# A retrieval trunk's gate one-hots and gate products: one one-hot moved from GpSimd to VectorE, multiplies and loads of gates placed by tile

## The chip, the cores and the metric

The kernel runs on one core of a Trainium2 chip. The metric is the device time of one execution in microseconds (us). Engines are named as in the profile: PE (TensorE, with PEld for its weight loads), DVE (VectorE), ACT (ScalarE), POOL (GpSimd) and SP (SyncE, whose queue SPq issues most transfers). Each engine works through its own queue in order; engines wait for each other by semaphores.

## What is computed

Two layers over 512 tokens of 1024 channels, in float32. Each layer has a mixing part (a convolution module with gated linear attention, then forgetting attention) and an expert-retrieval part (PEER), which this change touches. Of the reference:

```python
PEER_HEADS, PEER_NKEYS, PEER_TOPK = 8, 128, 16      # 128 x 128 = 16384 experts
def peer_ffn(h, wq, keys, u, v):
    ...
    sc, j = lax.top_k(cand, PEER_TOPK)
    e1 = jnp.take_along_axis(i1, j // PEER_TOPK, axis=-1)
    e2 = jnp.take_along_axis(i2, j % PEER_TOPK, axis=-1)
    experts = e1 * PEER_NKEYS + e2
    gates = jax.nn.softmax(sc, axis=-1)
    ...
    def block(args):
        ht, et, gt = args
        act = jax.nn.gelu(jnp.einsum('td,ted->te', ht, u[et]), approximate=False)
        return jnp.einsum('te,ted->td', gt * act, v[et])
```

Every token picks 128 experts (8 heads, 16 each). An expert has a number `e1 * 128 + e2`, a row of `u` that is dotted with the token, and a row of `v` that is added with the weight gate times gelu(dot).

## The kernel before

The 512 tokens are four blocks of 128. Block 0 is done by gathering: its 128 `u` rows per token come by indirect transfers that POOL issues (`g_u`, L861, a [128, 1024] tile `gr` each, one per slot), DVE dots them with `h` (L863); later the `v` rows come the same way (`g_v`, L872) and DVE adds them to `x` with their weights (L874). The other three blocks (384 tokens, `TD`) are done densely: all 16384 experts are computed, as 128 expert tiles of 128 (index `e1`, `NE1`), and a dense gate matrix, zero where a token did not pick an expert, masks them.

**u steps** (`u_step`). For one tile of 128 experts the weight tile `raw` (512 KB) is loaded by SP into one of 4 buffers. Matmuls are done with a high and a low half: ACT makes the high half `whi` (L50), DVE the low half `wlo` (L51), three buffers each. PE then does 8 x 3 matmuls `pu` (L77 to L79) against the tokens' own halves; ACT takes the gelu (L853). The last 24 tiles' activations stay in SBUF (`act0` and so on), the other 104 are put by in DRAM (`aside`).

**The gate stage.** From u step 36 to 116, `gate4` makes the dense gates, four tokens at a time, 96 times a layer. For a token, the matrix [e2, e1] is the product of two one-hot matrices over its 128 slots. DVE makes the one-hots over e2 of four tokens at once (`a2`, L898, [128, 512]). The four gate-weighted one-hots over e1 (`a1`, [128, 128] each) are shared out: POOL makes tokens 0 and 1 and DVE token 2 (L901), ACT token 3 with two activations (L904, L905). PE multiplies them (L911, behind a u step's matmuls; six groups of four fall to five u steps), ACT copies the result into `big` (L912), and for every 16 tokens SP writes `big` to `G` in DRAM (L914, 1 MB). `a1` and `a2` have three buffers. In the same stretch POOL issues about 1.4 row gathers for each u step, five buffers `gr`.

**The v sweep.** For tile n (0 to 127, the 24 with kept activations first) `prepare` loads and splits the `v` weights as above and makes the weights per token: gates `gc`, a block of 1.5 MB for 8 tiles (L957, two buffers), times the activations (L969, [128, 384], in place), split into `wh` (ACT) and `wl` (DVE). The activations that were put by return as `at`, two tiles a load (L960, three buffers). PE does 18 matmuls `acc` (L1025) a tile. `fetch(n)` issues the loads of `gc` and `at`; the sweep calls it AHEAD = 4 tiles before their use.

**What sets the order.** The program is written in this sequence, but a scheduler with a simulated timeline decides where each instruction stands in its engine's queue, as soon as its operands and buffers are free by that simulation. `tc.issue_after(x)` adds an edge: what is traced inside stands behind `x` on that engine. `self.last_lo` is the last low half that `split` made.

Of the kernel before, what the change touches and what calls it, by code (L numbers as in the profile page):

```python
# [4 lines left out]
F32 = mybir.dt.float32  # L5
# [6 lines left out]
ALU = mybir.AluOpType  # L12
# [4 lines left out]
P = 128  # L17
# [5 lines left out]
NE1 = 128  # L23
# [6 lines left out]
TG = 16  # L30
NTG = TD // TG
EC = 8
KEEP = 24
ROWS = 5
LAG = 2
AHEAD = 4
# [8 lines left out]
class Trunk:  # L45
# [768 lines left out]
    def peer_body(self, L, hT, h0, sp, sb):  # L814
        nc, tc, A = self.nc, self.tc, self.A
# [4 lines left out]
        G = self.dp.tile([NTG, P, NE1 * TG], F32, name="G")  # L820
# [12 lines left out]
        def pump(q, n):  # L833

            done = []
            for _ in range(min(int(n), len(q))):
                f, args = q.pop(0)
                done.append(f(*args))
            return [f for f in done if f]


        def u_step(e, eng=None):
            wh, wl = self.weight(uT[e], (KD, P), eng)
            if e % 2 and HEADS * WQU <= e < NE1 - 2:
                p = self.bank([P, TD], "pu")
            else:
                p = self.ps.tile([P, TD], F32, tag="b", name="pu", bufs=2)
            lo = self.last_lo
            for k in range(KD):
                mm = self.mm3(p, wh[:, k], wl[:, k], hD[0][:, k], hD[1][:, k], k == 0, k == KD - 1)  # L850
            put_by = e < NE1 - KEEP
            a = sb.tile([P, TD], F32, name="xact", bufs=3) if put_by else kept[e - (NE1 - KEEP)]
            self.last_gelu = nc.scalar.activation(a, p, AF.Gelu)  # L853
            if put_by:
                nc.sync.dma_start(aside[e], a)
            return lo, mm
# [27 lines left out]
        def flip(b):  # L884
            p = self.bank([P, 3, P])
            for j, t in enumerate((E[:, 0, DB[b]], E[:, 1, DB[b]], S[:, DB[b]])):
                nc.tensor.transpose(p[:, j], t.rearrange("p h k -> p (h k)"), self.ident)
            nc.scalar.activation(sT[b][:, 0:3], p, AF.Copy)
            nc.scalar.activation(sT[b][:, 3], p[:, 2], AF.Copy, scale=-1.0)

        def gate4(ub, b, tg, g):
            t0 = tg * TG + 4 * g
            if g == 0:
                self.big = ub.tile([P, NE1, TG], F32, name="big", bufs=2)
            a2 = ub.tile([P, 4, P], F32, name="a2", bufs=3)
            a1 = ub.tile([P, 4, P], F32, name="a1", bufs=3)
            e1, e2, gate, step = (sT[b][:, k, t0:t0 + 4] for k in range(4))
            nc.vector.tensor_tensor(a2, self.iota[:, None, :].to_broadcast([P, 4, P]),  # L898
                                    e2[:, :, None].to_broadcast([P, 4, P]), op=ALU.is_equal)
            for t in range(3):  # L900
                (nc.vector if t == 2 else nc.gpsimd).tensor_scalar(a1[:, t], self.iota, e1[:, t:t + 1], gate[:, t:t + 1],  # L901
                                                                   op0=ALU.is_equal, op1=ALU.mult)

            nc.scalar.activation(a1[:, 3], self.iota, AF.Abs, scale=-1.0, bias=e1[:, 3:4])  # L904
            nc.scalar.activation(a1[:, 3], a1[:, 3], AF.Relu, scale=step[:, 3:4], bias=gate[:, 3:4])  # L905
            big = self.big

            def multiply():
                p = self.bank([P, 4, P])
                for t in range(4):  # L910
                    nc.tensor.matmul(p[:, t], a2[:, t], a1[:, t], start=True, stop=True)  # L911
                nc.scalar.activation(big[:, :, g * 4:g * 4 + 4].rearrange("p e t -> p t e"), p, AF.Copy)  # L912
                if g == TG // 4 - 1:
                    nc.sync.dma_start(G[b * (P // TG) + tg], big.rearrange("p e t -> p (e t)"))  # L914

            return multiply
# [3 lines left out]
        with tc.tile_pool(name=f"pr{L}", bufs=2, reuse_waits="tile") as rb:  # L920
            for hd in range(HEADS):
                qT = []
                for w in range(2):
                    p = self.proj_T(A["wq"][L, 2 * hd + w], hT, nc.gpsimd if w and hd else None,
                                    after=None if hd else self.last_sq)
# [6 lines left out]
                for b in range(NB):  # L932
                    p = self.bank([P, 2, P])
# [13 lines left out]
        order = [*range(NE1 - KEEP, NE1), *range(NE1 - KEEP)]  # L947
        gcs, ats = {}, {}

        def fetch(n):  # L950

            if n >= NE1:
                return
            e = order[n]
            if n % EC == 0:
                gcs[n] = vb.tile([P, NTG, EC * TG], F32, name="gc")
                nc.sync.dma_start(gcs[n], G[:, :, e * TG:(e + EC) * TG].rearrange("g p n -> p g n"))  # L957
            if e < NE1 - KEEP and n % 2 == 0:
                ats[n] = vb.tile([P, 2, TD], F32, name="at", bufs=3)
                nc.sync.dma_start(ats[n], aside[e:e + 2].rearrange("e p t -> p e t"))  # L960

        def prepare(n):

            e, r = order[n], n % EC
            a = kept[e - (NE1 - KEEP)] if e >= NE1 - KEEP else ats[n - n % 2][:, n % 2]
            vh, vl = self.weight(vN[e], (2, 512))
            lo = self.last_lo
            w = gcs[n - r][:, :, r * TG:(r + 1) * TG]
            nc.vector.tensor_tensor(w, w, a.rearrange("p (g t) -> p g t", t=TG), op=ALU.mult)  # L969
            wh = vb.tile([P, TD], F32R, name="wh", bufs=3)  # L970
            wl = vb.tile([P, TD], F32R, name="wl", bufs=3)
            self.split(w, *[t.rearrange("p (g t) -> p g t", t=TG) for t in (wh, wl)])
            return lo, (n, vh, vl, wh, wl)
# [9 lines left out]
        vpool = tc.tile_pool(name=f"pv{L}", bufs=2, reuse_waits="tile")  # L983
        ub, vb = upool.__enter__(), None
        gates = [(gate4, (ub, b, tg, g)) for b, tg in groups for g in range(TG // 4)]
        while nu < NE1:
            if vb and nu == NE1 - 1:
                ready.append(prepare(0))
            lo, mm = u_step(nu)
            nu += 1  # L990
            with tc.issue_after(mm.ins):
                for f in products:
                    f()
                if nu == first:
                    for b in range(nd):
                        flip(b)
            products = []
            if nu >= first:
                cg += ng
                products = pump(gates, cg)  # L1000
                cg -= int(cg)
            if not (gates or products or vb):
                upool.__exit__(None, None, None)
                vb = vpool.__enter__()
                for n in range(AHEAD):
                    fetch(n)
            with tc.issue_after(lo.ins):
                for f in rows.pop(0):
                    f()
            cq += nq  # L1010
            rows.append(pump(gathers, cq))
            cq -= int(cq)
        assert vb and not (gates or products or gathers or any(rows))
        ready.append(prepare(1))
        g_w()

# [14 lines left out]
        for n in range(NE1):  # L1031
            fetch(n + AHEAD)
            lo, tile = ready.pop(0) if ready else prepare(n)
            tail.append(tile)
            if n < NE1 - 3:
                for b in range(nd):
                    v_sweep(tail, b)
                tail.clear()
            with tc.issue_after(lo.ins):
                for f in rows.pop(0):  # L1040
                    f()
            cq += nq
            rows.append(pump(gathers, cq))
            cq -= int(cq)
            if not gathers and not any(rows) and not done:
                done = True
                g_end()
# [124 lines left out]
```

## Time and profile before

| | |
|---|---|
| median of 3 runs | 3236.9 us (3230.26 to 3238.59) |
| the profiled execution | 3237.96 us |
| its span (first to last instruction) | 3236.2 us |
| mean granted PE clock | 0.985 |
| gate stage, layers 0 and 1 | from 543.9 and 2183.6 us on, first `L911` |
| v sweep, layers 0 and 1 | first `acc` matmuls at about 1045 and 2688, last at about 1585 and 3231 us |

The span holds everything between the first and the last instruction; 1.8 us of the execution lie outside it. Rows of the profile name a source line, an engine, an operation and output<-input by the program's names; `xN` is a count. In a table of windows each engine has its busy time in that stretch, then come the clock granted to PE (1.00 is full), the share of the 16 transfer engines that is busy, and GB/s. In a wait row the numbers are total us, times, longest. "Chain" is the work that ended last, followed back step by step to what released it.

### The profile page before, as it was taken

The page shows a single profiled execution, that of the slowest core. Times are in us where ns is not written, and L with a number is a line of the kernel's source. Part 1 is how long each engine was busy: PE and PEld are TensorE (multiplying, and loading weights), DVE is VectorE, ACT ScalarE, POOL GpSimd, SP SyncE. Part 2 cuts the span into 40 slices and gives each one's busy share as a digit, 9 for nine tenths or more (in the row PEclk, how much of TensorE's full clock was granted, in tenths as well). Part 3 has the DMA queues.
Part 4 walks back from the last instruction along what each step waited for, and adds up shares of the span by engine and source line. Part 5 has one row for each costly group of instructions (what it writes and reads, how often), then busy time and mean ns, then how long its engine had stood idle before and what let it go on. Part 6 is the DMA issues. An engine that isn't in the chain of part 4 may idle for free.

```text
span 3236.2 us, 45689 instructions
## 1 busy us (share of the span) xinstructions
PE 3112.4 (96%) x15932; PEld 2712.8 (84%) x15932; DVE 2361.4 (73%) x4744; ACT 1440.8 (45%) x2258; POOL 1416.7 (44%) x992
## 2 busy tenths in 40 slices
PE   8999999899999999999999999998999999999999
PEld 6768998899999788877766679998999998788787
DVE  7765988677676788878545639886776767788886
ACT  4353334566564333333356623345665643333333
POOL 1310124999994343333100001229999963443340
PEclk9999999999999999999999999998999999999999
DMA  4113445899899899999421124448998897999996
GB/s 153 57 37 123 145 138 188 310 325 329 307 326 308 277 343 373 359 334 347 143 79 46 33 90 143 139 164 283 334 321 313 308 319 273 325 369 353 350 350 215
DMA packets 334201, 787.15 MB, mean 243 GB/s; under 512 B 26745, under 2 KB 181770, under 8 KB 327826
## 3 DMA queue, kind: packets, MB, share of 16 engines
q1 hardware_dynamic: 260242, 515.76, 46.6%
q0 software_dynamic: 73728, 268.47, 23.4%
q8 instruction: 125, 2.05, 0.3%
q14 instruction: 106, 0.87, 0.1%
HBM read 687.59 MB, written 96.47 MB: 242 GB/s over the span
## 4 chain that ended last, share of the span: by engine, by line
PE 74%; POOL 9%; DMA 6%; DVE 5%; issue 4%; ACT 1%; DVEq 0%; POOLq 0%; SPq 0%; ACTq 0%
PE acc L1025 25%; PE pu L78 7%; PE pu L79 7%; PE pu L77 7%; POOL a L901 6%; PE bank L77 5%; PE bank L79 5%; PE bank L78 5%; DMA gc<-G 5%; PE bank L911 4%; POOL gr L861 3%; DVE wlo L51 1%; PE po L671 1%; PE pc L284 1%; PE bank L639 1%
## 5 line engine op out<-in xcount | busy, mean ns | idle before, releaser
L50 ACT ACTIVATE whi<-raw 128x1024 fp32r<-128x1024 f32 x604 | 636.0, 1057 | 860.3 <-PE pu L78 488.7
L51 DVE TENSOR_TENSOR wlo<-raw,whi 128x1024 fp32r<-128x1024 f32 x565 | 696.0, 1232 | 191.9 <-ACT whi L50 165.1
L77 PE MATMUL pu<-hhi,whi 128*128 128x384 f32 x2048 | 706.3, 345 | 1.0 <-ACT hhi L116 0.9
L79 PE MATMUL pu<-hhi,wlo 128*128 128x384 f32 x2048 | 694.0, 339 | 8.0 <-DVE wlo L51 8.0
L78 PE MATMUL pu<-hlo,whi 128*128 128x384 f32 x2048 | 692.6, 338 | 0.0
L872 POOL DMA_INDIRECT gr<-in_vF_dram,ids x256 | 383.6, 1499 | 671.9 <-DVE x L874 612.0
L901 POOL TENSOR_SCALAR a<-cst,sT 128x128 f32<-128x128 f32 x384 | 560.2, 1464 | 6.4
L1025 PE MATMUL acc<-wlo,wh 128*128 128x512 f32 x1536 | 476.7, 392 | 15.4 <-DVE wlo L51 15.4
L1025 PE MATMUL acc<-whi,wl 128*128 128x512 f32 x1536 | 475.6, 391 | 0.0
L1025 PE MATMUL acc<-whi,wh 128*128 128x512 f32 x1536 | 436.2, 390 | 8.9 <-ACT whi L50 8.9
L50 ACT ACTIVATE wh<-gc 128x384 fp32r<-128x384 f32 x256 | 134.2, 525 | 662.4 <-PE acc L1025 648.2
L79 PEld LDWEIGHTS pu<-hhi,wlo 128*128 128x128 f32 x2048 | 389.7, 190 | 9.5 <-DVE wlo L51 9.3
L77 PEld LDWEIGHTS pu<-hhi,whi 128*128 128x128 f32 x2048 | 391.0, 191 | 3.3 <-ACT hhi L116 1.4
L78 PEld LDWEIGHTS pu<-hlo,whi 128*128 128x128 f32 x2048 | 391.0, 191 | 1.9 <-DVE hlo L117 0.6
L861 POOL DMA_INDIRECT gr<-in_uN_dram,ids x256 | 318.2, 1243 | 122.8 <-DVE ids L944 55.3
L863 DVE CUSTOM_DVE_ANT_0 gr<-gr,h 128x1024 f32<-128x1024 f32 x256 | 311.7, 1233 | 67.6 <-DMA gr<-in_uN_dram,ids 67.4
L1025 PEld LDWEIGHTS acc<-wlo,wh 128*128 128x128 f32 x1536 | 289.3, 189 | 78.5 <-DVE wlo L51 18.7
L1025 PEld LDWEIGHTS acc<-whi,wh 128*128 128x128 f32 x1536 | 288.3, 188 | 72.1 <-ACT whi L50 12.2
L1025 PEld LDWEIGHTS acc<-whi,wl 128*128 128x128 f32 x1536 | 290.3, 189 | 60.7
L874 DVE SCALAR_TENSOR_TENSOR x<-gr,dots,x 128x1024 f32<-128x1024 f32 x256 | 327.4, 1279 | 0.4
L898 DVE TENSOR_TENSOR a<-cst,sT 128x512 f32<-128x512 f32 x192 | 134.5, 700 | 195.7 <-PE bank L911 190.6
L51 POOL TENSOR_TENSOR wlo<-raw,whi 128x1024 fp32r<-128x1024 f32 x39 | 99.0, 2539 | 398.5 <-ACT whi L50 398.5
(248 smaller groups left out, 4189.8 us busy)
## 6 DMA issues: line engine op xcount, KB each, us to landing
raw<-in_uT_dram SPq DMA_DIRECT2D x256, 512.0 KB
raw<-in_vF_dram SPq DMA_DIRECT2D x256, 512.0 KB
G<-big SPq DMA_DIRECT2D x48, 1024.0 KB
gc<-G SPq DMA_DIRECT2D x32, 1536.0 KB
aside<-xact SPq DMA_DIRECT2D x208, 192.0 KB
at<-aside SPq DMA_DIRECT2D x104, 384.0 KB
raw<-in_w_in_dram SPq DMA_DIRECT2D x32, 512.0 KB
raw<-in_wq_dram SPq DMA_DIRECT2D x32, 512.0 KB
```

Source lines behind the costliest of these rows:

```text
L50: first = self.nc.scalar.activation(hi, raw, AF.Copy)
L51: self.last_lo = (eng or self.nc.vector).tensor_tensor(lo, raw, hi.bitcast(F32), op=ALU.subtract)
L77: mm(out, lh, rh, start=first, stop=False)
L78: mm(out, lh, rl, start=False, stop=False)
L79: return mm(out, ll, rh, start=False, stop=last)
L861: nc.gpsimd.indirect_dma_start(out=r, out_offset=None, in_=uN, in_offset=bass.IndirectOffsetOnAxis(ap=ids[:, s:s + 1], axis=0))
L863: return lambda: nc.vector.tensor_tensor_reduce(r, r, h0, 1.0, 0.0, ALU.mult, ALU.add, accum_out=dots[:, s:s + 1])
L872: nc.gpsimd.indirect_dma_start(out=r, out_offset=None, in_=vF, in_offset=bass.IndirectOffsetOnAxis(ap=ids[:, s:s + 1], axis=0))
L874: return lambda: nc.vector.scalar_tensor_tensor(self.x0, r, dots[:, s:s + 1], self.x0, op0=ALU.mult, op1=ALU.add)
L898: nc.vector.tensor_tensor(a2, self.iota[:, None, :].to_broadcast([P, 4, P]), e2[:, :, None].to_broadcast([P, 4, P]), op=ALU.is_equal)
L901: (nc.vector if t == 2 else nc.gpsimd).tensor_scalar(a1[:, t], self.iota, e1[:, t:t + 1], gate[:, t:t + 1], op0=ALU.is_equal, op1=ALU.mult)
L1025: nc.tensor.matmul(acc[b][c], wt[:, s], vt[:, c], start=(n == 0 and wt is wh and vt is vh), stop=(n == NE1 - 1 and wt is wl))
```

## The change

Three edits, all in `peer_body`; both layers run them.

1. In `gate4`, POOL makes the one-hot of token 0 only; tokens 1 and 2 are DVE's.
2. In `prepare`, the multiply of gates with activations gets an edge: it stands behind the low half that was made last before this tile (`lo0`, which in the sweep is `wl` of the tile before).
3. `fetch(n)` issues the gate block of tile n + 4 and the put-by activations of tile n, so gate blocks are asked for 8 tiles before their use instead of 4. When the v pool opens, `fetch` runs from -4 to 3 instead of 0 to 3.

```diff
             for t in range(3):
-                (nc.vector if t == 2 else nc.gpsimd).tensor_scalar(a1[:, t], self.iota, e1[:, t:t + 1], gate[:, t:t + 1],
-                                                                   op0=ALU.is_equal, op1=ALU.mult)
+                (nc.vector if t else nc.gpsimd).tensor_scalar(a1[:, t], self.iota, e1[:, t:t + 1], gate[:, t:t + 1],
+                                                              op0=ALU.is_equal, op1=ALU.mult)
...
         def fetch(n):
-            if n >= NE1:
-                return
-            e = order[n]
-            if n % EC == 0:
-                gcs[n] = vb.tile([P, NTG, EC * TG], F32, name="gc")
-                nc.sync.dma_start(gcs[n], G[:, :, e * TG:(e + EC) * TG].rearrange("g p n -> p g n"))
-            if e < NE1 - KEEP and n % 2 == 0:
+            m = n + AHEAD
+            if m % EC == 0 and m < NE1:
+                e = order[m]
+                gcs[m] = vb.tile([P, NTG, EC * TG], F32, name="gc")
+                nc.sync.dma_start(gcs[m], G[:, :, e * TG:(e + EC) * TG].rearrange("g p n -> p g n"))
+            if 0 <= n < NE1 and (e := order[n]) < NE1 - KEEP and n % 2 == 0:
...
+            lo0 = self.last_lo
             vh, vl = self.weight(vN[e], (2, 512))
             lo = self.last_lo
             w = gcs[n - r][:, :, r * TG:(r + 1) * TG]
-            nc.vector.tensor_tensor(w, w, a.rearrange("p (g t) -> p g t", t=TG), op=ALU.mult)
+            with tc.issue_after(lo0.ins):
+                nc.vector.tensor_tensor(w, w, a.rearrange("p (g t) -> p g t", t=TG), op=ALU.mult)
...
-                for n in range(AHEAD):
+                for n in range(-AHEAD, AHEAD):
                     fetch(n)
```

What the scheduler makes of it, at three places. Numbers behind names tell buffers apart.

DVE in the middle of layer 0's gate stage, before: for each group of four tokens the one-hots `a2`, one `a1`, then a u step's low half and a dot of a gathered row (its second row reads the sum out).

```order
L898 TENSOR_TENSOR a2_7627<-cst_77,sT1_2046 128x512
L901 TENSOR_SCALAR a1_7628<-cst_77,sT1_2046 128x128
L51 TENSOR_TENSOR wlo_7651<-raw_7648,whi_7650 128x1024
L863 ISA gr_7585,dots_2044<-gr_7585,h0_1933 128x1024
L863 ISA dots_2044 128x1
L898 TENSOR_TENSOR a2_7636<-cst_77,sT1_2046 128x512
```

And after the change:

```order
L898 TENSOR_TENSOR a2_7627<-cst_77,sT1_2046 128x512
L901 TENSOR_SCALAR a1_7628<-cst_77,sT1_2046 128x128 x2
L51 TENSOR_TENSOR wlo_7651<-raw_7648,whi_7650 128x1024
L863 ISA gr_7585,dots_2044<-gr_7585,h0_1933 128x1024
L863 ISA dots_2044 128x1
L898 TENSOR_TENSOR a2_7636<-cst_77,sT1_2046 128x512
```

The second one-hot stands directly behind the first, ahead of the same low half; the rest of the sequence is unmoved here. On POOL the same rows stand with one `L901` for every two.

DVE in the v sweep of layer 0, where the third block of gates (tiles 16 to 23) comes in; before (the first three of its eight multiplies, the others follow without a gap):

```order
L51 TENSOR_TENSOR wl_9987<-gc_9849,wh_9986 128x384
L51 TENSOR_TENSOR wlo_9982<-raw_9979,whi_9981 128x1024
L874 SCALAR_TENSOR_TENSOR x0_72<-gr_9945,dots_2044,x0_72 128x1024
L969 TENSOR_TENSOR gc_10109<-gc_10109,act16_2064 128x24x16
L969 TENSOR_TENSOR gc_10109<-gc_10109,act17_2065 128x24x16
L969 TENSOR_TENSOR gc_10109<-gc_10109,act18_2066 128x24x16
```

After the change, the same block's first multiplies:

```order
L51 TENSOR_TENSOR wl_10216<-gc_9745,wh_10215 128x384
L971 TENSOR_TENSOR gc_9979<-gc_9979,act16_2064 128x24x16
L51 TENSOR_TENSOR wlo_10211<-raw_10208,whi_10210 128x1024
L874 SCALAR_TENSOR_TENSOR x0_72<-gr_10174,dots_2044,x0_72 128x1024
L51 TENSOR_TENSOR wl_10250<-gc_9979,wh_10249 128x384
L971 TENSOR_TENSOR gc_9979<-gc_9979,act17_2065 128x24x16
L51 TENSOR_TENSOR wlo_10245<-raw_10242,whi_10244 128x1024
```

Before, all eight multiplies of a block stood in a row, behind tile 8's work, with seven tiles still ahead of the first one's use; now one stands in each tile, between the `wl` of the tile before it and that tile's `wlo`. At the start of the sweep the first block's multiplies stood ahead of the low half of the fifth last u step; now the first one stands behind the low half of the second last.

SP in layer 0, where the fourth block of gates (tiles 24 to 31) is asked for, before:

```order
L58 DMA raw_10304<-in_vF_dram 128x1024
L957 DMA gc_10368<-G_2038 128x24x128
L58 DMA raw_10336<-in_vF_dram 128x1024
L58 DMA raw_10372<-in_vF_dram 128x1024
L960 DMA at_10571<-aside_2039 128x2x384
L960 DMA at_10639<-aside_2039 128x2x384
L960 DMA at_10705<-aside_2039 128x2x384
```

And after:

```order
L58 DMA raw_10306<-in_vF_dram 128x1024
L957 DMA gc_10240<-G_2038 128x24x128
L58 DMA raw_10338<-in_vF_dram 128x1024
L58 DMA raw_10372<-in_vF_dram 128x1024
L58 DMA raw_10404<-in_vF_dram 128x1024
```

The gate load stands between the `raw` of tiles 18 and 19 in both. The loads of `at` stood three in a row behind it; now they come one by one, the next of them ahead of the `raw` of tile 28.

## The prediction

> **What bounds the kernel now.** I read the page's totals and the chain that ended last first, then the table of windows, then who PE waits for, then the groups of the costly stage.
>
> ```profile
> PE 3112.4 (96%) x15932; PEld 2712.8 (84%) x15932; DVE 2361.4 (73%) x4744; ACT 1440.8 (45%) x2258; POOL 1416.7 (44%) x992
> PE 74%; POOL 9%; DMA 6%; DVE 5%; issue 4%; ACT 1%; DVEq 0%; POOLq 0%; SPq 0%; ACTq 0%
> PE acc L1025 25%; PE pu L78 7%; PE pu L79 7%; PE pu L77 7%; POOL a L901 6%; PE bank L77 5%; PE bank L79 5%; PE bank L78 5%; DMA gc<-G 5%; PE bank L911 4%; POOL gr L861 3%; DVE wlo L51 1%; PE po L671 1%; PE pc L284 1%; PE bank L639 1%
> ```
>
> PE is busy nearly always, yet 9% of the chain is POOL (one-hots, L901, and row gathers, L861) and 5% the load of gates `gc<-G`. POOL's 44% over the whole span says nothing; by stage:
>
> ```profile
> core 0: us, PE busy (x) PEld busy (x) DVE busy (x) ACT busy (x) POOL busy (x), PEclk, DMA share, GB/s
> 540.00:1000.00 460.00, 436.14 (x2705) 429.85 (x2705) 326.04 (x511) 271.52 (x451) 428.08 (x315) 0.98 0.90 314
> 900.00:980.00 80.00, 80.00 (x515) 80.00 (x514) 60.80 (x97) 50.20 (x85) 75.07 (x59) 1.00 0.89 320
> 1000.00:1060.00 60.00, 55.16 (x292) 52.50 (x292) 37.35 (x57) 23.08 (x33) 14.27 (x11) 0.97 0.85 287
> 1060.00:1200.00 140.00, 134.33 (x584) 110.11 (x583) 106.69 (x127) 48.57 (x64) 56.33 (x34) 0.99 0.93 321
> 1200.00:1580.00 380.00, 373.62 (x1636) 307.55 (x1635) 307.63 (x361) 137.28 (x184) 126.89 (x90) 1.00 0.96 336
> 2180.00:2640.00 460.00, 434.93 (x2684) 427.20 (x2683) 323.63 (x508) 270.37 (x448) 431.51 (x313) 0.98 0.89 310
> 2640.00:2700.00 60.00, 56.66 (x303) 54.18 (x302) 36.73 (x54) 20.79 (x32) 14.15 (x11) 0.97 0.88 300
> 2700.00:2840.00 140.00, 134.41 (x578) 110.01 (x577) 105.53 (x126) 49.25 (x66) 54.72 (x34) 0.98 0.92 315
> 2840.00:3220.00 380.00, 373.42 (x1641) 307.55 (x1642) 308.60 (x362) 136.47 (x183) 128.38 (x89) 1.00 0.95 336
> ```
>
> In the gate stage (540 to 1000 in layer 0, 2180 to 2640 in layer 1) POOL is busy 428 of 460 us, 93%, and PE is idle 24 us. PE's waits in these two stages are all on POOL; behind them, up to 1240 and 2860, on DVE's low halves:
>
> ```profile
> PE bank L911 <- POOL a L901: 23.4, 23, 5.3
> PE bank L911 <- POOL a L901: 24.7, 28, 4.9
> ...
> PE acc L1025 <- DVE wlo L51: 5.7, 3, 3.9
> PE pu L79 <- DVE wlo L51: 4.8, 2, 3.5
> ```
>
> **Step 1, one one-hot off POOL.** How much the POOL waits really cost is more than their idle time, because the clock drops behind a long one. These are slices of 1 us at the end of layer 0's 5.3 us wait and 3 us behind it; the granted clock (third number from the right) is down to half, while PE works:
>
> ```profile
> 609.00:610.00 1.00, 0.00 (x0) 0.00 (x0) 1.00 (x3) 0.00 (x0) 1.00 (x2) 0.75 0.87 266
> 613.00:614.00 1.00, 1.00 (x6) 1.00 (x5) 0.73 (x2) 0.73 (x1) 1.00 (x2) 0.50 1.13 458
> ```
>
> So I count by periods instead. Six gate products stand among five u steps, and in the stretch without a wait that pattern repeats at
>
> ```profile
> 917.33 1.78 PE bank L911 x16
> 943.49 1.78 PE bank L911 x16
> 969.65 1.78 PE bank L911 x16
> ...
> L911 PE MATMUL bank<-a,a x768: 272/275/582, 543.9 to 996.4; 128*128 128x128 f32 x192
> L911 PE MATMUL bank<-a,a x768: 272/275/583, 2183.6 to 2639.9; 128*128 128x128 f32 x192
> ```
>
> that is 26.16 us. From the first to the last of 96 products there are 95/6 periods, 414.2 us at full pace. Measured: 452.5 and 456.3 us. The excess is 38.3 + 42.1 = 80.4 us. That is all this edit can win. The groups of layer 0's stage say why POOL is short:
>
> ```profile
> L901 POOL TENSOR_SCALAR a<-cst,sT 128x128 f32<-128x128 f32 x192 | 277.4, 1450 | 3.2
> L861 POOL DMA_INDIRECT gr<-in_uN_dram,ids x123 | 152.0, 1236 | 29.0 <-issue 18.7 <-DVE dots L863 7.4 <-DVE a L901 2.1
> L898 DVE TENSOR_TENSOR a<-cst,sT 128x512 f32<-128x512 f32 x95 | 66.4, 699 | 91.0 <-PE bank L911 91.0
> L901 DVE TENSOR_SCALAR a<-cst,sT 128x128 f32<-128x128 f32 x95 | 34.0, 358 | 0.0
> ```
>
> A period holds 12 POOL one-hots of 1.45 us and some 7 gathers of 1.24 us plus about 0.15 of issue each: 27.1 us, over PE's 26.16. With 6 one-hots it is 18.4. POOL loses 96 x 1.45 = 139 us a layer, 428 to 289, so PE at 26.16 becomes the bound. DVE takes 96 x 0.358 = 34 us: in the full-pace stretch, 60.8 of 80 us becomes 67.4, 84%. What hides it is the 91 us that DVE waits for PE to free an `a2`; uncovered it would cost 34 us a layer. I leave 6 us a layer for the start, where five gathers still stand ahead of POOL's first one-hot, and 4 for friction (DVE waiting for a gathered row, denser transfers). These two are choices. Their lower bound is nothing; the upper one comes from the transfers: if they stuck at a share of 0.93, as from 1060 to 1200, the stage could not fall under 460 x 0.90/0.93 = 445 us, a gain of 15 a layer. At 0.96, which the sweep holds for 380 us, it is 29 a layer, so I stay near there. **Gain 80.4 - 20 = 60 us**, bounds 30 to 80.
>
> [...] The trace bears out that something stretches POOL:
>
> ```profile
> L901 POOL TENSOR_SCALAR a<-cst,sT x384: 783/1306/3972, 543.0 to 2634.2; 128x128 f32<-128x128 f32 x192
> L901 DVE TENSOR_SCALAR a<-cst,sT x192: 333/342/464, 539.6 to 2625.7; 128x128 f32<-128x128 f32 x192
> ```
>
> [...]
>
> **Step 2, the multiplies and the gate loads.** Before, DVE has eight multiplies of a gate block in a row and waits in front of them while low halves stand behind:
>
> ```profile
> 1018.77 3.84 DVE L969 TENSOR_TENSOR gc<-gc,act 128x384 f32<-128x384 f32 x8 [5.11 <-DMA gc<-G]
> 1022.52 1.22 DVE L51 TENSOR_TENSOR wlo<-raw,whi 128x1024 fp32r<-128x1024 f32 x1
> 1031.22 1.07 ACT L50 ACTIVATE whi<-raw 128x1024 fp32r<-128x1024 f32 x1 [8.69 <-DMA raw<-in_uT_dram]
> 1120.42 1.50 DVE L969 TENSOR_TENSOR gc<-gc,at 128x384 f32<-128x384 f32 x3 [8.90 <-DMA gc<-G]
> 1105.60 14.80 DMA gc<-G
> ...
> DVE gc L969 <- DMA gc<-G: 69.7, 16, 9.1
> ```
>
> Afterwards each multiply stands one tile ahead of its use. On SP the block of 16 tiles later still stands where its buffer comes free (between the same two `raw` loads as before): the earlier call in the code changes nothing there. What removes the wait is that the first multiply comes about eight tiles, some 32 us, behind the issue, against the 14.8 us that this one took to land. Places where PE lost: 1060 to 1200 idle 5.7 plus clock 1% of 140, 7.1 us; 2700 to 2840 5.6 plus 2%, 8.4; of these 15.5 I take 13. At the handover (idle 4.8 and 3.3) only 3 of 8.2 go: `whi` of the third last u step waits for its `raw` until 1031.2, behind two gate loads and three of activations on SP, and that is unchanged. **Gain 16 us**, bounds 8 to 24. In the rest of the sweep PE is idle 6.4 and 6.6 us; DVE's gate waits feed part of it by late `raw` issues. I take **3**, bounds -10 (transfers are already at 0.96 there) and 13.
>
> What covers the multiply in its new place, ahead of the tile's `wlo`, is idle time that DVE has in a tile of 4.08 us (1142.40 to 1146.48; the last row is the multiply's own mean over the sweep):
>
> ```profile
> 1142.40 0.56 DVE L51 TENSOR_TENSOR wl<-gc,wh 128x384 fp32r<-128x384 f32 x1 [0.67 <-ACT wh L50]
> 1143.39 1.23 DVE L51 TENSOR_TENSOR wlo<-raw,whi 128x1024 fp32r<-128x1024 f32 x1 [0.43 <-ACT whi L50]
> 1146.48 0.56 DVE L51 TENSOR_TENSOR wl<-gc,wh 128x384 fp32r<-128x384 f32 x1 [0.67 <-ACT wh L50]
> ...
> L969 DVE TENSOR_TENSOR gc<-gc,at 128x384 f32<-128x384 f32 x104 | 51.5, 552 | 23.7 <-DMA gc<-G 23.7
> ```
>
> 0.43 us is free just there, 1.10 in the tile; a multiply takes 0.48 (eight in 3.84) to 0.55. Queued behind it are `wlo` and the `x0` row; PE needs that `wlo` two tiles later, so 0.1 us more costs nothing. The loads of `at` also come later, but ahead of a `raw` that is itself four tiles ahead.
>
> **Sum.** 60 + 16 + 3 = 79 us from the profiled execution's 3237.96 (its span 3236.2; median of the runs 3236.9): **3159 us**. All upper bounds, 80 + 24 + 13 = 117, give 3121; all lower, 30 + 8 - 10 = 28, give 3210.
>
> **Rivals.**
> - Transfers or gathered rows become the bound of the gate stage. For: a share of 0.90 in 460 us would be 0.98 in 424. Against: 900 to 980 runs at full pace with 0.89. Step 1 then gives its lower bound of 30, step 2 its 8, the sweep nothing: 3200.
> - Step 2 does nothing, since PE's short waits come from `raw` that lands late: step 1 alone, 3178. For: unchanged SP rows; against: the 8.9 us wait directly ahead of PE's 3.9.
> [...]
> - Slower: in the sweep the multiply adds to the tile instead of filling DVE's idle 1.10 us, because `wl` and `wlo` slip with it. Price 0.55 x 256 = 141 us against gains of 79: 3300. It decides once DVE's tile is longer than 4.08 + 79/256 = 4.39 us. Against it: the sum of DVE's work in a tile, 0.56 + 0.55 + 1.23 + 1.28, is 3.6 us.
>
> **Chances.** Forecast 0.66; transfers bind 0.14; step 2 void 0.08; POOL still bound 0.04; no change by gains and losses that cancel 0.03; slower 0.05. A measurement of this kernel tells about 0.3% from no change, so faster 0.91, same 0.04, slower 0.05. The range takes the first three cases and the upper bounds: 3125 to 3208.
>
> **What would show it.** Step 1 right: no PE wait on POOL above 2 us a layer, POOL near 290 us in the stage, first to last product near 424 us, no clock slices of 0.5 there. Wrong: PE waits on DVE's one-hots or `wlo` in that stage. Step 2 right: DVE's wait for `gc` under 10 us (69.7 now), PE idle from 1060 on near nothing; wrong: DVE tiles over 4.08 us, or ACT waiting longer for `raw`.

## The result, and the profile after

| | before | after |
|---|---|---|
| median | 3237.74 us (4 runs, 3230.26 to 3248.78) | 3147.97 us (4 runs, 3147.10 to 3148.14) |
| the profiled execution, its span | 3237.96, 3236.2 us | 3148.14, 3146.3 us |
| ratio | | 0.972, 95% interval 0.9691 to 0.9748 |

The change is faster by 89.8 us, 2.8%; 3159 was forecast, in a range from 3125 to 3208. The page after the change, engine totals and the chain that ended last:

```profile
PE 3080.9 (98%) x15932; PEld 2696.8 (86%) x15932; DVE 2406.8 (76%) x4936; ACT 1437.2 (46%) x2258; POOL 1155.1 (37%) x800
PE 90%; DVE 3%; DMA 2%; issue 1%; ACT 1%; SPq 1%; POOL 1%; DVEq 0%; ACTq 0%; POOLq 0%
PE acc L1027 33%; PE pu L79 10%; PE pu L78 10%; PE pu L77 10%; PE bank L77 5%; PE bank L79 5%; PE bank L78 5%; PE bank L911 5%; PE po L671 1%; PE pc L284 1%; PE bank L639 1%; PE bank L935 1%; DVE wlo L51 1%; SPq L960 1%; POOL gr L861 1%
```

PE's share of the chain rises from 74% to 90%, POOL's falls from 9% to 1%, and `gc<-G` is gone from it. The windows of the gate stage, the handover and the sweep, of both layers (columns as before):

```profile
540.00:960.00 420.00, 417.46 (x2665) 416.34 (x2665) 344.17 (x604) 267.44 (x451) 333.94 (x217) 1.00 0.94 341
960.00:1013.00 53.00, 48.52 (x269) 47.61 (x268) 25.71 (x36) 19.59 (x28) 13.92 (x10) 0.94 0.95 321
1013.00:1545.00 532.00, 527.37 (x2328) 435.84 (x2327) 434.86 (x520) 196.24 (x265) 153.25 (x126) 1.00 0.94 329
2140.00:2556.00 416.00, 414.68 (x2659) 413.85 (x2658) 343.32 (x603) 266.41 (x447) 329.27 (x216) 1.00 0.95 343
2556.00:2609.00 53.00, 48.31 (x265) 47.48 (x264) 25.23 (x34) 16.34 (x24) 13.66 (x10) 0.94 0.94 316
2609.00:3141.00 532.00, 527.37 (x2327) 435.93 (x2327) 432.47 (x512) 192.06 (x256) 151.30 (x123) 1.00 0.93 327
```

PE has under 3 us of idle time in a gate stage. PE is still idle for 4.5 and 4.7 us in the two handovers, with a granted clock of 0.94. For a balance I take the first and the last start of the gate products (L911) and of the sweep's high-half matmuls (L1025, now L1027), first of the sweep before the change, then of both after it:

```profile
L1025 PE MATMUL acc<-whi,wh x768: 387/389/500, 1045.2 to 1588.2; 128*128 128x512 f32 x192
L1025 PE MATMUL acc<-whi,wh x768: 387/389/628, 2687.4 to 3230.2; 128*128 128x512 f32 x192
```

```profile
L911 PE MATMUL bank<-a,a x768: 272/275/377, 545.4 to 963.7; 128*128 128x128 f32 x192
L911 PE MATMUL bank<-a,a x768: 272/275/377, 2143.6 to 2559.4; 128*128 128x128 f32 x192
L1027 PE MATMUL acc<-whi,wh x768: 387/389/504, 1012.4 to 1543.8; 128*128 128x512 f32 x192
L1027 PE MATMUL acc<-whi,wh x768: 387/389/504, 2609.0 to 3140.3; 128*128 128x512 f32 x192
```

| stretch, us | before | after | difference |
|---|---|---|---|
| up to the first gate product | 543.9 | 545.4 | +1.5 |
| gate stages | 452.5 + 456.3 | 418.3 + 415.8 | -74.7 |
| handovers (last product to first sweep matmul) | 48.8 + 47.5 | 48.7 + 49.6 | +2.0 |
| sweeps | 543.0 + 542.8 | 531.4 + 531.3 | -23.1 |
| layer 0's sweep to layer 1's gates | 595.4 | 599.8 | +4.4 |
| behind the last sweep | 6.0 | 6.0 | 0 |

The sum is -89.9 us, the difference of the spans. Four questions follow: which edit won what; what holds the handover; whether DVE is close to becoming the bound; and what the 4.4 us between the layers are.

### The profile page after: what moved, and what is told of

Its sections match the earlier page's. It is cut to its first block, busy times and chain, and to the rows that moved or that the text cites. A ratio compares the mean times of both kernels' runs of the same rounds, so it can differ in the third digit from the quotient of the medians.

```text
span 3146.3 us, 45733 instructions
## 1 busy us (share of the span) xinstructions
PE 3080.9 (98%) x15932; PEld 2696.8 (86%) x15932; DVE 2406.8 (76%) x4936; ACT 1437.2 (46%) x2258; POOL 1155.1 (37%) x800
## 4 chain that ended last, share of the span: by engine, by line
PE 90%; DVE 3%; DMA 2%; issue 1%; ACT 1%; SPq 1%; POOL 1%; DVEq 0%; ACTq 0%; POOLq 0%
PE acc L1027 33%; PE pu L79 10%; PE pu L78 10%; PE pu L77 10%; PE bank L77 5%; PE bank L79 5%; PE bank L78 5%; PE bank L911 5%; PE po L671 1%; PE pc L284 1%; PE bank L639 1%; PE bank L935 1%; DVE wlo L51 1%; SPq L960 1%; POOL gr L861 1%
## 5 line engine op out<-in xcount | busy, mean ns | idle before, releaser
L872 POOL DMA_INDIRECT gr<-in_vF_dram,ids x256 | 317.7, 1241 | 717.7 <-DVE x L874 658.7
L1027 PE MATMUL acc<-wlo,wh 128*128 128x512 f32 x1536 | 472.7, 389 | 0.0
L1027 PE MATMUL acc<-whi,wl 128*128 128x512 f32 x1536 | 472.5, 389 | 0.0
L1027 PE MATMUL acc<-whi,wh 128*128 128x512 f32 x1536 | 436.5, 390 | 9.3 <-ACT whi L50 9.3
L861 POOL DMA_INDIRECT gr<-in_uN_dram,ids x256 | 352.5, 1377 | 237.6 <-DVE dots L863 140.7
L1027 PEld LDWEIGHTS acc<-whi,wh 128*128 128x128 f32 x1536 | 287.6, 188 | 72.1 <-ACT whi L50 12.6
L1027 PEld LDWEIGHTS acc<-wlo,wh 128*128 128x128 f32 x1536 | 288.3, 188 | 60.0
L1027 PEld LDWEIGHTS acc<-whi,wl 128*128 128x128 f32 x1536 | 288.3, 188 | 59.8
L901 POOL TENSOR_SCALAR a<-cst,sT 128x128 f32<-128x128 f32 x192 | 330.6, 1722 | 13.2 <-PE bank L911 4.9
L51 DVE TENSOR_TENSOR wl<-gc,wh 128x384 fp32r<-128x384 f32 x256 | 142.7, 558 | 179.4 <-ACT wh L50 170.0
```

What stands on the lines that cost most here:

```text
L51: self.last_lo = (eng or self.nc.vector).tensor_tensor(lo, raw, hi.bitcast(F32), op=ALU.subtract)
L861: nc.gpsimd.indirect_dma_start(out=r, out_offset=None, in_=uN, in_offset=bass.IndirectOffsetOnAxis(ap=ids[:, s:s + 1], axis=0))
L872: nc.gpsimd.indirect_dma_start(out=r, out_offset=None, in_=vF, in_offset=bass.IndirectOffsetOnAxis(ap=ids[:, s:s + 1], axis=0))
L901: (nc.vector if t else nc.gpsimd).tensor_scalar(a1[:, t], self.iota, e1[:, t:t + 1], gate[:, t:t + 1], op0=ALU.is_equal, op1=ALU.mult)
L1027: nc.tensor.matmul(acc[b][c], wt[:, s], vt[:, c], start=(n == 0 and wt is wh and vt is vh), stop=(n == NE1 - 1 and wt is wl))
```

## The experiments

### Each edit alone

The first, the second and the third edit, each alone on the kernel before.

```diff
 # e1: gate4 only
-                (nc.vector if t == 2 else nc.gpsimd).tensor_scalar(...)
+                (nc.vector if t else nc.gpsimd).tensor_scalar(...)
 # e2: prepare only
+            lo0 = self.last_lo
...
+            with tc.issue_after(lo0.ins):
+                nc.vector.tensor_tensor(w, w, a.rearrange(...), op=ALU.mult)
 # e3: fetch only
-            if n % EC == 0:
+            m = n + AHEAD
+            if m % EC == 0 and m < NE1:
...
-                for n in range(AHEAD):
+                for n in range(-AHEAD, AHEAD):
```

> The kernel before with the first edit alone (POOL makes one one-hot of four). My theory (POOL's queue was the bound of the gate stage, and the three edits add up by stage): first to last gate product 415 to 419 us in both layers (452.5 and 456.3 before, 418.3 and 415.8 after the whole change), the sweep as before (first to last acc matmul 543 us), so 3237.7 - 75 = about 3163 us. Rival (the gate stage only gets faster because the sweep's start no longer disturbs it, or DVE is short without the new order): gate stage above 430 us, time above 3180.

> The kernel before with the second edit alone (the edge that puts each multiply behind the wl of the tile before). My theory (the row of eight multiplies, waiting for its gate block on DVE, cost PE the time): sweep 531 us in both layers, DVE's wait for gc near 0, gate stage as before (452 to 457 us), time 3237.7 - 21 = about 3217. Rival (the earlier call for gate blocks is what matters): sweep 540 us or more, time above 3230.

> The kernel before with the third edit alone (fetch asks for gate blocks four tiles sooner in the code). My theory (the block can't leave before its buffer is free, and the scheduler already put it there): time as before, 3238 within 0.3%, sweep 543 us, DVE's wait for gc 60 to 75 us. Rival (the blocks do come sooner): DVE's wait for gc under 35 us and 3217 to 3225 us.

| kernel | median us | ratio to before, interval | gate stages | sweeps |
|---|---|---|---|---|
| before (16 runs) | 3238.2 | | 452.5, 456.3 | 543.0, 542.8 |
| e1, one-hot | 3167.87 | 0.9786 (0.9759 to 0.9813) | 418.5, 419.1 | 543.4, 541.9 |
| e2, edge | 3220.87 | 0.9947 (0.9932 to 0.9963) | 450.8, 454.9 | 531.3, 531.4 |
| e3, fetch | 3237.56 | 1.0003 (0.9990 to 1.0017) | 450.9, 459.9 | 539.3, 542.6 |

The stages come from these rows, two of e1's gate products and two of e2's sweep:

```profile
L911 PE MATMUL bank<-a,a x768: 272/275/377, 544.6 to 963.1; 128*128 128x128 f32 x192
L911 PE MATMUL bank<-a,a x768: 272/275/377, 2152.3 to 2571.4; 128*128 128x128 f32 x192
```

```profile
L1027 PE MATMUL acc<-whi,wh x768: 387/389/504, 1043.3 to 1574.6; 128*128 128x512 f32 x192
L1027 PE MATMUL acc<-whi,wh x768: 387/389/504, 2676.6 to 3208.0; 128*128 128x512 f32 x192
```

The first two edits act each in its own stage, and their gains add up: 70.3 + 17.3 = 87.6 of 89.8 us. The third does nothing to the time: layer 0's sweep is 3.7 us shorter in e3's profile, but the medians agree. In e3 DVE waits for gate blocks as before (69.7 us there):

```profile
DVE gc L969 <- DMA gc<-G: 63.3, 13, 8.9
```

In e2, as in the changed kernel, the wait of DVE for `gc` isn't among its waits any more, with the blocks asked for at the old place in the code. PE's waits for low halves in the sweeps, in the kernel before

```profile
PE acc L1025 <- DVE wlo L51: 15.4, 8, 4.0
```

are gone in e2 too, and its sweeps of 531.3 and 531.4 us are those of the whole change. So the sweep's gain is the second edit's. That it comes from the multiplies no longer standing in a row is the nearest reading, as PE waited for `wlo` and DVE, ahead of it, for `gc`; but the edge also spreads the loads of `at`, which stood three in a row on SP, and no run separates the two. e1's sweep is as long as before: the one-hots play no part in it.

### What holds the handover

```diff
-        nc.sync.dma_start(raw, src)
+        self.last_raw = nc.sync.dma_start(raw, src)
...
-                nc.sync.dma_start(gcs[m], G[...])
+                with tc.issue_after(self.last_raw.ins):
+                    nc.sync.dma_start(gcs[m], G[...])
...
-                nc.sync.dma_start(ats[n], aside[...])
+                with tc.issue_after(self.last_raw.ins):
+                    nc.sync.dma_start(ats[n], aside[...])
```

> The changed kernel with one edge more on SP: gate blocks and put-by activations stand behind the raw load that was issued last in the program, so that the second gate block and the first three loads of at no longer stand ahead of the last u steps' raw loads at the handover to the sweep. My theory (PE's 4.4 us idle there and the halved clock behind it come from a raw that stands behind 4 MB of other loads on SP): ACT's wait for raw at the handover under 1 us, last gate product to first acc matmul 43 us instead of 48.7 and 49.6, time 3148 - 12 = about 3136. Rival (the transfers as a whole are short there, whatever their order): wait 3 us or more, or a new wait of DVE for gc or at early in the sweep, time 3146 to 3152.

In the changed kernel, ACT's row of the `whi` that PE waits for, and PE's two slices of 10 us around it:

```profile
1000.34 1.06 ACT L50 ACTIVATE whi<-raw 128x1024 fp32r<-128x1024 f32 x1 [6.75 <-DMA raw<-in_uT_dram]
```

```profile
990.00:1000.00 10.00, 7.23 (x42) 6.91 (x40) 0.00 (x0) 0.49 (x1) 0.97 (x2) 0.97 1.06 382
1000.00:1010.00 10.00, 8.30 (x35) 7.79 (x36) 6.19 (x9) 8.28 (x10) 1.95 (x1) 0.69 0.71 230
```

and SP's queue ahead of it, where the second number is the time that the issues themselves took:

```profile
970.75 6.08 SPq L957 DMA_DIRECT2D gc<-G  x2
976.88 13.76 SPq L960 DMA_DIRECT2D at<-aside  x3
990.69 0.94 SPq L58 DMA_DIRECT2D raw<-in_uT_dram  x2
```

SP is stuck for 20 us in issuing two gate blocks and three loads of `at`; the `raw` behind them leaves at 990.7. The first block is needed at the start of the sweep, but the second only 8 tiles into it and the loads of `at` 24 tiles. In e4, where only the first block still goes ahead of that `raw`, the same slices read

```profile
990.00:1000.00 10.00, 10.00 (x59) 10.00 (x58) 4.31 (x9) 5.83 (x8) 1.04 (x1) 1.00 1.06 338
1000.00:1010.00 10.00, 10.00 (x57) 9.70 (x57) 4.88 (x7) 3.82 (x6) 0.00 (x0) 1.00 0.74 245
```

PE is busy throughout at full clock, ACT has no wait for a `raw` there, and the handovers take 41.7 us each (962.8 to 1004.5, 2549.8 to 2591.5), 14.9 us less in all. The median is 3131.0 us, ratio to before 0.9675 (0.9649 to 0.9701). It was the order on SP and not the amount of transfers.

### How close DVE is, and what stretches POOL

e5 gives DVE token 0's one-hot too, so POOL makes none. e6 gives token 1's to ACT, e7 all three to POOL. All on the changed kernel.

```diff
 # e5
-                (nc.vector if t else nc.gpsimd).tensor_scalar(...)
+                nc.vector.tensor_scalar(...)
 # e6: for t in (0, 2) as in the changed kernel, and
+            for t in (1, 3):
+                nc.scalar.activation(a1[:, t], self.iota, AF.Abs, scale=-1.0, bias=e1[:, t:t + 1])
+                nc.scalar.activation(a1[:, t], a1[:, t], AF.Relu, scale=step[:, t:t + 1], bias=gate[:, t:t + 1])
 # e7
-                (nc.vector if t else nc.gpsimd).tensor_scalar(...)
+                nc.gpsimd.tensor_scalar(...)
```

> The changed kernel with token 0's one-hot on DVE as well, so that POOL makes none and DVE three of four. It takes the cover off: DVE gets 96 x 0.342 = 33 us a layer more in the gate stage, 344 to 377 of 418 us. My theory (DVE has room, it waits 119 us over both layers for PE to free an a2, and PE stays the bound): gate stage 416 to 421 us, that wait down to 50 to 80 us, time 3148 within 0.4%. Rival (DVE is the next bound right behind POOL): PE waits for DVE's one-hots or wlo in the gate stage by over 5 us a layer, gate stage above 426 us, time above 3162.

> The changed kernel with token 1's one-hot made by ACT (the two activations that make token 3's) instead of DVE: POOL keeps one of four, DVE one, ACT two. It asks why POOL's one-hot went up from 1450 to 1769 ns in the gate stage. Theory A (the tensor_scalar that was moved to DVE holds POOL): POOL's one-hot is back at 1500 ns or less. Theory B (it is the denser rest of DVE's work, above all its operations with two inputs from SBUF, or POOL's rows falling together with them): it stays at 1650 ns or more. Time in both 3148 within 0.4%, as ACT has 267 of 420 us busy there and takes 96 x 0.88 = 84 more.

> The changed kernel with all of tokens 0, 1 and 2 on POOL: a dose against the idea that POOL's queue sets the period when it is over PE's 26.16 us. Theory: a period of 18 one-hots of 1.45 us and 7.03 gathers of 1.24 + 0.15 us is 35.9 us, so 95/6 of them make a gate stage of 568 us and the time is 3148 + 2 x 150 = about 3450 us (3400 to 3500). With two on POOL the same sum gave 27.2 us, 430 us, where 452 and 456 were measured, so the sum may be 5% short: 596 us, 3505. Rival (the stage is set by PE's wait for single late one-hots, not by the sum of POOL's queue): below 3380.

| kernel | one-hots of four on POOL, DVE, ACT | median us | ratio to before, interval | gate stages |
|---|---|---|---|---|
| e7 | 3, 0, 1 | 3417.51 | 1.0554 (1.0522 to 1.0586) | 543.3, 548.0 |
| before | 2, 1, 1 | 3238.01 | | 452.5, 456.3 |
| changed | 1, 2, 1 | 3147.97 | 0.972 (0.9691 to 0.9748) | 418.3, 415.8 |
| e6 | 1, 1, 2 | 3144.67 | 0.9709 (0.9693 to 0.9725) | 419.0, 417.4 |
| e5 | 0, 3, 1 | 3136.99 | 0.9691 (0.9675 to 0.9707) | 415.4, 415.1 |

e7 tests the idea of POOL's queue with a larger dose. The sum of its queue gave 568 us, and 543.3 and 548.0 were measured, from these rows of the gate products:

```profile
L911 PE MATMUL bank<-a,a x768: 270/275/582, 545.2 to 1088.5; 128*128 128x128 f32 x192
L911 PE MATMUL bank<-a,a x768: 270/275/583, 2269.6 to 2817.6; 128*128 128x128 f32 x192
```

The one-hot took 1301 ns in layer 0 of e7 and not the 1450 of the sum. With 1301 the sum gives 525 us, 3% under the measured time, as the 430 for two one-hots is 5% under 452.5. So POOL's queue sets the stage, and its sum comes out a few per cent short.

In e5 only one PE wait is left in layer 0's gate stage (first fence), and DVE still waits 42.6 us there for PE (its own waits, second fence):

```profile
PE pu L79 <- DVE wlo L51: 0.6, 1, 0.6
```

```profile
DVE a L898 <- PE bank L911: 42.6, 59, 1.4
```

So DVE isn't next to the bound: it took 96 more one-hots a layer, and PE's stage became no longer. Its wait for a free `a2` fell to 83.2 us over both layers, where 50 to 80 was expected. Whether e5 is faster than the changed kernel isn't settled: the intervals overlap, and of its 11 us some 9 lie ahead of the gate stage (541.6 against 545.4) and between the layers (594.7 against 599.8). The first of these isn't the edit's either, as e8, with the same one-hots, starts its products at 544.8. The gate stages alone add up to 830.5 us in e5 and 830.7 in e8, against 834.1 to 837.9 in the four kernels with one one-hot on POOL (the changed kernel, e1, e4 and e6): 3 to 7 us, from one profile of each.

e6 was to say why POOL's one-hot grew. POOL's groups from 560 to 960, first of the changed kernel, then of e6, which has half the `tensor_scalar` on DVE:

```profile
L901 POOL TENSOR_SCALAR a<-cst,sT 128x128 f32<-128x128 f32 x91 | 162.0, 1781 | 6.4 <-PE bank L911 2.7 <-issue 0.9
```

```profile
L901 POOL TENSOR_SCALAR a<-cst,sT 128x128 f32<-128x128 f32 x92 | 159.5, 1735 | 12.1 <-PE bank L912 8.1 <-issue 1.7
```

It stays at 1735 ns: the moved instruction isn't what stretches POOL's one-hot. A small part of the growth is a matter of which one-hot stayed: in the kernel before, the first of POOL's two took 1514 ns and the second 1415, over both layers. The last section sets them beside DVE's work.

### Both additions together

e8 is the changed kernel with e4's edge and e5's one-hots.

> The changed kernel with both additions that won: all of tokens 0 to 2 on DVE (3137.0 alone) and the SP edge that lets the last u steps' raw go ahead of the second gate block (3131.0 alone). They act in different places, the gate stage and its start, and the handover, so if gains add up by stage: 3148 - 11 - 17 = 3120 us (3115 to 3126), gate stage 415 us, handover 42 us. Rival (what e5 gained is chance of the clock between the layers, 595 against 600 us there, and the start of the gate stage): 3127 to 3134 us.

The median is 3124.51 us (3122.55 to 3125.5), ratio to before 0.9648 (0.9631 to 0.9665): 3.5% under the kernel before, and clear of the changed kernel's interval, though not of e4's. Gate stages 416.1 and 414.6 us, handovers 41.7 and 41.8 us. Of the gain of 23.5 us over the changed kernel 14.8 are the handovers.

## Why the prediction was right, and where its sizes were off

- **Gate stage.** The mechanism held: POOL's queue, over PE's period with two one-hots, under it with one. The gain is 74.7 us where 60 was said. The term that was off is the allowance of 10 us a layer for start and friction: of the excess of 80.4 us, 5.7 stay in all. The friction did not come: the transfers rose to a share of 0.94 and 341 GB/s, under the 0.98 that the first rival worked out. PE's waits on POOL, one of the signs, fell from 48.2 to 1.8 us over both layers.
- **The load of POOL** was off the other way: 334 us busy in 420, not near 290. Its one-hot rose from 1450 to 1769 ns, 31 us a layer, and its row gathers from 1236 to 1358 ns, 12 us more; the last section takes up the one-hots. It didn't show in the time, as POOL was 86 us from the bound.
- **What the moved `tensor_scalar` does to POOL.** Between the two rows of e6's section, the second with half the `tensor_scalar` on DVE, the one-hot differs by 46 ns, 4.4 us a layer. POOL's gathers take 1358 ns in the changed kernel's stage and 1275 in e6's, 10 us a layer; but in e5, with more `tensor_scalar` on DVE and no one-hot on POOL, they take 1215, so what stretches them stays open.
- **DVE's cover** was there: 344 of 420 us is 82%, 84% was said for the stretch at full pace; the wait for a free `a2` fell from 190.6 to 118.9 us over both layers and in e5 to 83.2.
- **The sweep.** 23.1 us came, against 13 + 3. Set against each other matmul by matmul, the two kernels show 8.1 and 9.5 us of it up to tile 36 (1204.5 and 2848.1 before the change), the stretch for which 13 was said, and 3.5 and 2.0 after it, where 3 was said. PE's idle time is 15.0 of the 23.1 us; with the rest the granted clock rose from 0.99 to 1.00, and that share the sum took too low. The statement that the third edit changes nothing is borne out by e3. DVE's wait for `gc`, a sign that was to fall under 10 us, is gone. The multiply fits into DVE's idle time as said, against the rival of a slower sweep; a tile of the changed kernel is still 4.08 us (1143.52 to 1147.60), with the wait ahead of `wlo` gone:

```profile
1143.52 0.56 DVE L51 TENSOR_TENSOR wl<-gc,wh 128x384 fp32r<-128x384 f32 x1 [0.67 <-ACT wh L50]
1143.99 0.55 DVE L971 TENSOR_TENSOR gc<-gc,at 128x384 f32<-128x384 f32 x1
1144.51 1.23 DVE L51 TENSOR_TENSOR wlo<-raw,whi 128x1024 fp32r<-128x1024 f32 x1
1147.60 0.56 DVE L51 TENSOR_TENSOR wl<-gc,wh 128x384 fp32r<-128x384 f32 x1 [0.67 <-ACT wh L50]
```

- **The handover** is the step that failed: 3 us were to be won, 2 were lost. That `raw` is late behind the gate and `at` loads was read rightly, and e4 shows it; but I counted the removed DVE waits as a gain in front of it. PE waited there 4.8 and 3.2 us for `wlo` before and 4.2 and 4.4 us for `whi` after, with the granted clock down from 0.97 and 0.96 to 0.93: it met the same late load, which left 27.7 us behind layer 0's last gate product before and 27.0 after. The sign named for this, a longer wait of ACT for `raw`, didn't tell: that wait went from 8.69 to 6.75 us.
- **Nowhere in the sum** were the 5.9 us lost outside the touched stages (+1.5 and +4.4).
- **Luck in the total.** 89.8 us against 79: the gate stage and the sweep gave 14.7 and 7.1 us more than said, the handover 5 us less, and the 5.9 us went the other way, so misses in both directions partly cancel. The upper bounds add up to 3121 us in the sum, where the stated range ends at 3125.

## What to carry to other kernels

An engine that is 44% busy over the span can be the bound of a stage, as POOL was, at 93% there: sum up its queue over one period of the stage's pattern and set it against PE's period. When one wait goes, ask what already lies ready behind it at the same place; here it was a load in an issue queue behind others that were needed much later, and in e4 its place was worth 14.9 us of the two handovers. Asking for a load earlier in the code is no earlier load where the scheduler places it by its buffer's release: e3 took 3237.56 us against 3238.2, and DVE waited 63.3 us for gate blocks against 69.7.

## What the runs showed of the hardware

**POOL's one-hots beside DVE's operations with two inputs.** POOL's shortest one-hot takes 780 ns, its longest 4.0 us. A few rows of the changed kernel, first POOL's, then DVE's at the same time:

```profile
898.30 2.35 POOL L901 TENSOR_SCALAR a<-cst,sT 128x128 f32<-128x128 f32 x1
901.89 1.12 POOL L901 TENSOR_SCALAR a<-cst,sT 128x128 f32<-128x128 f32 x1
```

```profile
897.62 1.22 DVE L51 TENSOR_TENSOR wlo<-raw,whi 128x1024 fp32r<-128x1024 f32 x1
898.76 1.22 DVE L863 CUSTOM_DVE_ANT_0 gr<-gr,h 128x1024 f32<-128x1024 f32 x1
...
901.55 0.69 DVE L898 TENSOR_TENSOR a<-cst,sT 128x512 f32<-128x512 f32 x1 [1.57 <-PE bank L911]
902.16 0.60 DVE L901 TENSOR_SCALAR a<-cst,sT 128x128 f32<-128x128 f32 x2
902.68 1.22 DVE L51 TENSOR_TENSOR wlo<-raw,whi 128x1024 fp32r<-128x1024 f32 x1
```

The first one-hot ends at 900.65, 0.67 us behind the end of DVE's dot (899.98), which has two inputs from SBUF as the `wlo` ahead of it. The second ends at 903.01, 0.77 us behind the end of the `a2` (902.24), and DVE's two `tensor_scalar` and the next `wlo` run into it at their usual length. All 192 one-hots of the changed kernel fit this. The nine that fall beside no operation of DVE with two inputs take 0.79 us on average, although a `tensor_scalar` of DVE runs beside eight of them; and in each of the others at most 0.80 us is left when the time beside such operations is taken off. The kernel before (384 one-hots, at most 0.83 us left) and e7 (576, 0.81) show the same. So in these three traces a POOL one-hot is longer by about the time that DVE's operations with two inputs run beside it, which fits e6; it is read from traces, and no run took those operations away. Whether DVE is held in its turn they don't settle: the changed kernel's `wlo` take 1.22 us on average beside a one-hot and 1.23 without one, those of the kernel before 1.26 and 1.22.

DVE's `tensor_scalar` takes longer at times, next to another part of POOL's work. In the changed kernel its row reads

```profile
L901 DVE TENSOR_SCALAR a<-cst,sT x384: 332/342/945, 540.3 to 2545.4; 128x128 f32<-128x128 f32 x192
```

where the longest took 464 ns before. 18 of the 384 take 0.68 to 0.95 us, and each of these ends within 0.23 us behind the end of one of POOL's row gathers. None is over 0.5 us in e5 or e6 (longest 442 and 401 ns). No run was made to find the cause.

**One wait, two clocks.** The 4.4 us between the layers lie mostly in one place. PE waits 2.1 us for the same activation in both kernels; slices of 8 us around that wait, before:

```profile
1632.00:1640.00 8.00, 5.88 (x29) 4.75 (x28) 3.40 (x5) 1.54 (x3) 0.00 (x0) 1.00 0.21 68
```

and after, with the wait itself from PE's waits (us in all, count, longest) in a fence behind it:

```profile
1588.00:1596.00 8.00, 6.01 (x17) 4.84 (x18) 3.27 (x5) 1.22 (x2) 0.00 (x0) 0.62 0.21 69
```

```profile
PE bank L590 <- ACT sq L614: 2.1, 1, 2.1
```

The granted clock stays at 1.00 in one and is 0.62 in the other, 0.38 x 8 = 3.0 us; set against each other matmul by matmul, the two kernels drift apart by 3.1 us there. Over all ten profiles the stretch between the layers takes from 593.4 (e4) to 599.8 us (the changed kernel), without order by what was edited. A wait of 2.1 us came with a full clock in one kernel and with 0.62 in the other; what decides between the two wasn't shown, as no run moved that wait alone. For differences below some 5 us of this kernel it is a reason to compare stages and not times.
